# One-core, two-block transformer kernel: inputs laid out on the host, first transfers reordered, idle matmuls at the start

## The chip, the cores and the metric

The kernel runs on one core of one Trainium2 chip. The metric is device time in microseconds (us) of one execution; lower is better.

## The reference, cut to what matters

Two transformer blocks of two layers each run one after the other on one sequence of 256 tokens with 1024 features, all in float32. Layer by layer they use different mixers:

```
x = first_block(x, ...)    # layer 0: MoBA + forgetting attention; layer 1: differential + sliding-window
return second_block(x, mem_2, ...)   # layer 0: MLA, layer 1: stick-breaking; each + cross attention + MLP

h = rmsnorm(x, norm_gain[layer])
proj = h @ w_in_ab[0]                # 1024 x 4104: q,k,v,gate (4 x 512) twice, and 8 forget columns
...
h = h + mem_cross_attn(rmsnorm_2(h, norm_cross[i]), rmsnorm_2(mem, norm_mem[i]), w_q, w_kv, w_o)
h = h + sq_relu_mlp(rmsnorm_2(h, norm_mlp[i]), mlp_w_in[i], mlp_w_out[i])
```

With 256 tokens every weight is read once and used for 256 rows, so the kernel streams 155 MB of weights through the core while the matrix engine works on them.

## The kernel before, in words

The whole program is first described as a list of operations (`describe`, L1667), then `Plan.schedule` (L261) plays it through with a table of assumed costs and fixes, for each engine and for the DMA queue on SP, the order in which instructions are issued. Nothing of that model runs on the chip: there each engine works through its row and waits at semaphores for its inputs and for buffers to come free.

Activations live transposed, as eight chunks of 128 features by 256 tokens. To come near float32 with the faster `fp32r` matmul, every operand is split into a high part `hi` (a rounding copy) and a low part `lo = raw - hi`, and a product is three matmuls: hi·hi, hi·lo, lo·hi. A weight piece is 128 x 1024 float32 (512 KB). `wtiles` (L636) asks for it, `wpiece` (L619) loads it into a buffer `raw` of the pool `k4`, and `split` (L632) makes hi (mostly on ScalarE) and lo (on VectorE). `k4` has five buffers, three for `raw` and two for `fraw` (the pieces of `mem_kv`); the plan lends them to each other. A piece feeds 12 matmuls with 512 columns (token-major outputs, `proj_tok`) or 24 with 256 (feature-major, `proj_feat`). VectorE's `lo` is the last reader of `raw`, so it frees the buffer for the next load.

Source rows: a piece takes 512 columns of two 128-row chunks, so a partition receives two runs of 2 KB. The pieces of `xa_w_kv_2` (`mem_kv`, L1455) have runs of 512 B and 1 KB.

`setup` (L740) loads x token-major in four tiles `xin` and the first gain vector as eight rows, turns both around with matmuls against the identity, and takes the sum of squares with ScalarE (`squares`, L817). Sixteen transposes make x; `mem_setup` (L1430) does the same for the memory (16 more). The other gain vectors come through `rows_T` (L727): one small load per vector into rows, then one transpose. `forget` (L1118) loads the eight forget columns as 1024 runs of 32 bytes. In `describe` order: `setup`, `layer_ab`, `setup_late`, `setup_rope`, `mem_setup`, then the next layers; with loads ready from the start, the plan is free to issue those of the late setups early.

DMAs are issued from SP in one row. The program hands the completion semaphores out in turn; there are eight (DMAHW0 to DMAHW7), and from the ninth transfer on a DMA waits for the transfer that last used its semaphore.

The lines in which the buffers are set:

```python
POOLS = {"k4": (1024, 5), "k2": (512, 33), "r2": (512, 46), ...
TAGS = {"raw": ("k4", 3), "fraw": ("k4", 2), "hi": ("r2", 12), "lo": ("r2", 16), ...
```

Of the kernel before, what the change touches and what calls it, by code (L numbers as in the profile page):

```python
# [165 lines left out]
class Plan:  # L166
    def __init__(self, nc):
        self.nc = nc
        self.ops, self.tags, self.pools = [], {}, {}
# [91 lines left out]
    def schedule(self):  # L261
# [19 lines left out]
        for b in {b for o in ops for b in o.news}:  # L281
            self.tags[b.tag]["pool"].use[b.first:b.last + 1] += 1
# [36 lines left out]
        while n < len(ops):  # L319
# [69 lines left out]
            if o.kind == "dma_start":  # L389
# [4 lines left out]
                o.start, o.end = t, st + d + 1500  # L394
# [71 lines left out]
class _Eng:  # L466
# [5 lines left out]
    def __getattr__(self, method):  # L472
        plan, e = self.plan, self.e

        def call(*args, deps=(), **kw):
# [3 lines left out]
            for p in deps:  # L479
# [86 lines left out]
WEL = 1024  # L566
SUB = 512
# [13 lines left out]
PREFER = {"A": 0.0, "V": 800, "G": 1000000.0}  # L581


class Net:
# [34 lines left out]
    def wpiece(self, src, f, pat, fill="", parts=1, **kw):  # L619
# [3 lines left out]
        self.nc.sync.dma_start(raw.rearrange(pat, **kw), src)  # L623
# [12 lines left out]
    def wtiles(self, w, k0, nk, c0, nc_, fill=""):  # L636
# [3 lines left out]
        while k < k0 + nk:  # L640
# [5 lines left out]
            for hi, lo in self.wpiece(w[k * 128:(k + n) * 128, c0:c0 + nc_].rearrange("(c p) n -> p c n", p=128),  # L646
                                      n * nc_, "p (c n) -> p c n", fill, n // m, c=n):
# [91 lines left out]

    def setup(self):  # L740
        nc, a = self.nc, self.a
        rows = self.t2([8, 128], "rows")
        xin = [[self.t2([128, 512], "xin") for _ in range(2)] for _ in range(NT)]
        nc.boost = 4e4
        nc.sync.dma_start(rows, a["norm_gain"].rearrange("l (c p) -> (l c) p", p=128)[0:8])
        for hf in range(2):
            nc.boost = 1e4 if hf else 3e4
            for t in range(NT):
                nc.sync.dma_start(xin[t][hf], a["x"][0, t * 128:(t + 1) * 128, hf * 512:(hf + 1) * 512])
# [13 lines left out]
        p = self.ps("T")  # L763
        nc.tensor.transpose(p[:, :8], rows, self.ident[:8, :8])
        g0 = self.sm([128, 8], "g0")
        nc.vector.tensor_copy(g0, p[:, :8])

        self.x = self.new_x()
        self.xt = self.new_T()
        for c0 in range(0, NC8, 2):  # L770
            p = self.ps("T").rearrange("p (c n) -> p c n", c=2)
            for t in range(NT):
                for c in range(2):
                    self.tr(p[:, c, t * 128:(t + 1) * 128],
                                xin[t][c0 // 4][:, (c0 % 4 + c) * 128:(c0 % 4 + c + 1) * 128])
            for c in range(2):
                self.evac_split(self.xt[0][c0 + c], self.xt[1][c0 + c], p[:, c], g0[:, c0 + c:c0 + c + 1])
            self.copy(self.x[c0 // 2], p)
        self.stats_x(self.squares(xin))
# [25 lines left out]

        parts = []
        for i, n in enumerate("qk"):
            for j, m in enumerate(("moba", "fox", "diff", "swa")):
                gg = a[f"{m}_{n}_gain"]
                parts.append((4 * i + j, bass.AP(tensor=gg.tensor, offset=gg.offset,  # L810
                                                 ap=[[64, 1], [0, 2], [1, 64]]), 1, "p (r d) -> p r d"))
        g64 = self.rows_T("sm", 8, parts)
        self.gqk = self.sm([128, 4], "gqk")
        nc.vector.scalar_tensor_tensor(self.gqk, g64[:, 0:4], 0.125, g64[:, 4:8], op0=OP.mult, op1=OP.mult)
        self.bfor = self.bc("bfor", "sm", a["b_forget"], 8)

    def squares(self, x):  # L817

        nc = self.nc
        s2 = self.sm([128, NT, 2], "ss2")  # L820
        for t in range(NT):
            for hf in range(2):
                nc.scalar.activation(self.t2([128, 512], "sq"), x[t][hf], AF.Square, accum_out=s2[:, t, hf:hf + 1])
        ss = self.sm([128, NT], "ss")
# [903 lines left out]
```

## Time and the profile before

| | |
|---|---|
| median of 3 runs | 967.68 us (966.92 to 969.37) |
| the profiled execution | 969.73 us, of which the span from first to last instruction is 968.0 us |
| TensorE busy in the span | 940.2 us (97%), 6829 matmul records |
| VectorE, ScalarE, GpSimd busy | 679.3, 573.7, 57.9 us |
| DMA | 154.89 MB read from HBM, mean 161 GB/s |

The profiled execution is 2.05 us above the median of the runs. A busy TensorE is not one at full pace: matmuls overlap, so the pace is read from how many follow each other in a stretch without idle time. A float32 (not fp32r) matmul appears as two records, a transpose as one.

### The profile page before, as it was taken

Reading aid. Unit: us, or ns where it says so; the run is one execution under the profiler, and the core shown is the slowest. Engines: PE = TensorE matmul, PEld = TensorE weight load, DVE = VectorE, ACT = ScalarE, POOL = GpSimd, SP = SyncE. Lnnn points to the kernel's source line nnn. Section 1 sums busy time; section 2 is a strip of 40 time slices with the busy share of each in tenths; the row PEclk is TensorE's granted clock in tenths of the full one; section 3 lists DMA queues with packets and bytes.
Section 4 is the critical chain, followed back from the end, with each engine's and each line's share of the span. In section 5 each row is a group of like instructions: output and inputs, shape, how many; then the busy total and the mean of one; then the engine's idle time right before and its main releaser. Section 6 shows DMA issues by size and latency. Waiting matters only on the chain.

```text
span 968.0 us, 18191 instructions
## 1 busy us (share of the span) xinstructions
PE 940.2 (97%) x6829; PEld 869.6 (90%) x6829; DVE 679.3 (70%) x1565; ACT 573.7 (59%) x1311; POOL 57.9 (6%) x96
## 2 busy tenths in 40 slices
PE   7899999999999999999999999999999999999997
PEld 5577889889989999999999999999899999999985
DVE  7689797797988857885555556846758776666654
ACT  5667784566777765874544546535756754444453
POOL 2214000041301100000000000000000000000000
PEclk9999999999999999999999999999999999999999
DMA  7987535644514534645455566446526355555641
GB/s 189 284 213 196 129 110 174 197 131 133 160 40 117 162 111 152 211 161 171 160 172 174 178 199 222 127 155 211 168 73 197 132 175 172 176 179 193 194 154 44
DMA packets 96677, 157.13 MB, mean 162 GB/s; under 512 B 9830, under 2 KB 28492, under 8 KB 96588
## 3 DMA queue, kind: packets, MB, share of 16 engines
q1 hardware_dynamic: 96236, 154.91, 51.7%
q0 software_dynamic: 352, 1.06, 0.4%
q8 instruction: 53, 0.87, 0.4%
q14 instruction: 36, 0.29, 0.1%
HBM read 154.89 MB, written 1.06 MB: 161 GB/s over the span
## 4 chain that ended last, share of the span: by engine, by line
PE 76%; DMA 12%; DVE 6%; ACT 3%; issue 1%; SPq 1%; POOL 1%; POOLq 0%; DVEq 0%; ACTq 0%
PE psum L552 76%; DMA k<-in_w_in_ab_dram 7%; DVE r L552 3%; DMA k<-in_mlp_w_out_dram 2%; DVE k L552 2%; ACT r L552 2%; ACT k L552 1%; DMA k<-in_sb_w_qkv_dram 1%; SPq L552 1%; POOL k L552 1%; DMA k<-in_xa_w_kv_dram 1%; DMA k<-in_mlp_w_in_dram 1%; DMA k<-in_xa_w_o_dram 0%; DMA k<-in_xa_w_q_dram 0%; DMA k<-in_mla_w_uq_dram 0%
## 5 line engine op out<-in xcount | busy, mean ns | idle before, releaser
L552 PE MATMUL psum<-r,r 128*128 128x256 f32 (+1 forms) x6018 | 882.8, 304 | 9.6 <-ACT r L552 7.9
L552 PEld LDWEIGHTS psum<-r,r 128*128 128x128 f32 x6018 | 794.2, 189 | 62.3 <-ACT r L552 12.0
L552 DVE TENSOR_TENSOR r<-k,r 128x512 fp32r<-128x512 f32 (+2 forms) x669 | 409.4, 649 | 147.9 <-ACT r L552 72.1
L552 ACT ACTIVATE r<-k 128x512 fp32r<-128x512 f32 (+3 forms) x567 | 311.2, 592 | 206.2 <-PE psum L552 100.4
L552 PE MATMUL psum<-k,k 128*128 128x128 f32 (+8 forms) x771 | 132.9, 307 | 11.2 <-DVE k L552 5.4
L552 ACT ACTIVATE k<-psum 128x256 f32<-128x256 f32 (+5 forms) x171 | 71.5, 453 | 111.2 <-PE psum L552 109.1
L552 PEld LDWEIGHTS psum<-k,k 128*128 128x128 f32 (+3 forms) x771 | 92.0, 166 | 27.3 <-DVE k L552 7.4
L552 POOL TENSOR_TENSOR k<-k,k 128x2 f32<-128x2 f32 (+3 forms) x42 | 48.7, 1173 | 861.6 <-DVE k L552 860.4
L552 ACT ACTIVATE k<-k 128x256 f32<-128x256 f32 (+4 forms) x149 | 72.1, 506 | 17.9 <-DVE k L552 13.9
L552 ACT ACTIVATE k<-k,k 128x128 f32<-128x128 f32 (+3 forms) x143 | 60.7, 448 | 11.0 <-DVE k L552 7.1
L552 DVE CAST r<-k 128x512 fp32r<-128x512 f32 (+2 forms) x102 | 40.7, 403 | 28.7 <-PE psum L552 10.3
L552 DVE TENSOR_TENSOR k<-psum,k 128x512 f32<-128x512 f32 (+2 forms) x53 | 33.4, 636 | 14.9 <-PE psum L552 14.8
L552 DVE TENSOR_TENSOR k<-k,k 128x512 f32<-128x512 f32 (+4 forms) x86 | 40.2, 480 | 1.6 <-ACT k L552 0.8
L552 ACT ACTIVATE r<-k,k 128x256 fp32r<-128x256 f32 x64 | 29.7, 500 | 18.4 <-DVE k L552 16.8
L552 DVE TENSOR_TENSOR k<-k 128x256 f32<-128x256 f32 (+3 forms) x38 | 12.9, 341 | 38.4 <-ACT k L552 38.2
L552 DVE SCALAR_TENSOR_TENSOR r<-k,k,r 128x256 fp32r<-128x256 f32 x72 | 34.4, 495 | 3.0 <-ACT r L552 2.1
L552 DVE TENSOR_TENSOR r<-psum,r 128x256 fp32r<-128x256 f32 (+1 forms) x52 | 24.0, 481 | 15.1 <-ACT r L552 14.7
L552 ACT ACTIVATE r<-psum 128x256 fp32r<-128x256 f32 (+1 forms) x49 | 20.9, 435 | 16.3 <-PE psum L552 15.7
L552 DVE TENSOR_SCALAR k<-k,k 128x8 f32<-128x8 f32 (+7 forms) x97 | 24.5, 281 | 5.0 <-POOL k L552 4.5
L552 ACT ACTIVATE k<-psum,k 128x512 f32<-128x512 f32 (+1 forms) x19 | 12.1, 650 | 6.7 <-PE psum L552 6.7
L552 DVE CUSTOM_DVE_ANT_0 k<-psum,k 128x256 f32<-128x256 f32 (+1 forms) x48 | 14.7, 352 | 1.0 <-PE psum L552 1.0
L552 ACT ACTIVATION_READ_ACCUMULATOR k<-k,k 128x1 f32 x80 | 15.2, 190 | 0.0
(40 smaller groups left out, 160.3 us busy)
## 6 DMA issues: line engine op xcount, KB each, us to landing
k<-in_mlp_w_in_dram SPq DMA_DIRECT2D x64, 512.0 KB, 4.4
k<-in_mlp_w_out_dram SPq DMA_DIRECT2D x64, 512.0 KB, 5.2
k<-in_w_in_ab_dram SPq DMA_DIRECT2D x32, 512.0 KB, 6.2
k<-in_w_in_cd_dram SPq DMA_DIRECT2D x26, 512.0 KB, 4.1
k<-in_sb_w_qkv_dram SPq DMA_DIRECT2D x24, 512.0 KB, 4.5
k<-in_xa_w_kv_dram SPq DMA_DIRECT2D x16, 512.0 KB, 5.6
k<-in_w_out_ab_dram SPq DMA_DIRECT2D x8, 512.0 KB, 3.7
k<-in_w_out_cd_dram SPq DMA_DIRECT2D x8, 512.0 KB, 4.5
```

What stands on the lines that cost most here:

```text
L552: return getattr(eng, method)(*[real(a) for a in args], **{k: real(v) for k, v in kw.items()})
```

## The change

- The host lays out x and the memory transposed in chunks of 128 features, so that both are loaded straight into their tiles; the 32 transposes, their copies and `squares` go. Sums of squares are now taken by `stats_sum`, as for every other norm; for the memory the factor 1/rms is applied to keys and values after their matmuls (`rmem_bc`, `rmem`).
- All gain vectors, the forget bias and the sinks come in one 128 x 110 array `consts`, by one DMA. `rows_T` goes, and 19 small loads with it.
- `Packed` records the weight pieces in the order in which the program asks for them, and the host writes each as one contiguous block: a partition receives one run of 4 KB (the forget columns one of 256 B).
- The plan's model: a DMA may be issued only up to 4 us (`AHEAD`) ahead of its modelled data, and lands 3.0 instead of 1.5 us after them. `gate` lets the loads of the memory, of `xa_w_kv_2`, of the forget columns and of a few constants be placed only behind the copies of the first key projection, and those of the final gain behind the copies in `x_tok`. These rules act on the order of issue alone.
- Six float32 matmuls on the iota tile `dj` stand first on TensorE; nothing reads their result.

```diff
@@ class Plan
+            if o.kind == "dma_start" and dma_free > t + AHEAD:
+                heapq.heappush(fut[e], (dma_free - AHEAD, c, i))
+                continue
...
-                o.start, o.end = t, st + d + 1500
+                o.start, o.end = t, st + d + 3000
...
-            for p in deps:
+            for p in deps if plan.gate is None or method != "dma_start" else (*deps, plan.gate):
...
+    def take(self, f, cut):
+        off = sum(128 * p[0] for p in self.pieces)
+        at = self.at
+        self.pieces.append((f, lambda w: cut(w[at])))
+        return bass.AP(tensor=self.ap.tensor, offset=self.ap.offset + off, ap=[[f, 128], [1, f]])
...
-        self.nc.sync.dma_start(raw.rearrange(pat, **kw), src)
+        self.nc.sync.dma_start(raw, w.take(f, cut))
...
@@ setup
-        rows = self.t2([8, 128], "rows")
-        xin = [[self.t2([128, 512], "xin") for _ in range(2)] for _ in range(NT)]
-        nc.boost = 4e4
-        nc.sync.dma_start(rows, a["norm_gain"].rearrange("l (c p) -> (l c) p", p=128)[0:8])
-        for hf in range(2):
-            nc.boost = 1e4 if hf else 3e4
-            for t in range(NT):
-                nc.sync.dma_start(xin[t][hf], a["x"][0, t * 128:(t + 1) * 128, hf * 512:(hf + 1) * 512])
+        cst = nc.tile([128, 110], "c128", "cst")
+        self.x = self.new_x()
+        nc.boost = 5e4
+        nc.sync.dma_start(cst, a["consts"])
+        for b in range(4):
+            nc.boost = (4e4, 1e4, 3e3, 3e3)[b]
+            nc.sync.dma_start(self.x[b], a["x"][:, 2 * b:2 * b + 2])
...
+        p = self.ps("T")
+        for i in range(WARM):
+            nc.tensor.matmul(p[:, 0:256], dj[:, 0:128], dj, start=True, stop=True)
...
-            self.copy(self.x[c0 // 2], p)
-        self.stats_x(self.squares(xin))
+        self.xt = self.gained(self.x, 0)
+        nc.boost = -2e4
+        self.stats_x()
...
@@ layer_ab
+                nc.gate = self.late = nc.seen
                 c, ncb = self.forget(w, xt)
+                nc.gate = None
...
@@ mem_setup
+        self.memT = [self.t2([128, 2, 256], "memT") for _ in range(4)]
+        for b in range(4):
+            nc.sync.dma_start(self.memT[b], self.a["mem_2"][:, 2 * b:2 * b + 2])
+        self.rmem = self.rms(self.memT)
+        self.rmem_bc = self.rstd_bc(self.rmem)
...
@@ mem_kv
-            self.evac_split(kT[0][b], kT[1][b], ps)
+            y = self.t2([128, 256], "xy")
+            self.nc.vector.tensor_tensor(y, ps, self.rmem_bc, op=OP.mult)
+            self.split(y, kT[0][b], kT[1][b])
```

SP's row at the start of the program, before: behind the loads of x and the first three weight pieces (128x2x512) stand the forget columns (128x8x8), the forget bias and seven gain vectors, with one weight piece among them. The names after "waits" are the semaphores that an entry waits for.

```order
L552 DMA k_90<-in_w_in_ab_dram 128x2x512
L552 DMA k_96<-in_w_in_ab_dram 128x2x512
L552 DMA k_100<-in_w_in_ab_dram 128x8x8 [waits DMAHW0_49]
L552 DMA k_104<-in_b_forget_dram 128x8 [waits DMAHW1_49]
L552 DMA k_106<-in_moba_q_gain_dram 1x2x64 [waits DMAHW2_49]
L552 DMA k_106<-in_fox_q_gain_dram 1x2x64 [waits DMAHW3_49]
L552 DMA k_106<-in_diff_q_gain_dram 1x2x64 [waits DMAHW4_49]
L552 DMA k_106<-in_swa_q_gain_dram 1x2x64 [waits DMAHW5_49]
L552 DMA k_106<-in_moba_k_gain_dram 1x2x64 [waits DMAHW6_49]
L552 DMA k_120<-in_w_in_ab_dram 128x2x512 [waits DMAHW7_49]
L552 DMA k_106<-in_fox_k_gain_dram 1x2x64 [waits DMAHW0_49]
L552 DMA k_106<-in_diff_k_gain_dram 1x2x64 [waits DMAHW1_49]
```

SP's row at the start of the program, of the change:

```order
L558 DMA k_64<-in_consts_dram 128x110
L558 DMA k_70<-in_x_dram 128x512
L558 DMA k_77<-in_w_in_ab_dram 128x1024
L558 DMA k_80<-in_x_dram 128x512
L558 DMA k_83<-in_w_in_ab_dram 128x1024
L558 DMA k_87<-in_x_dram 128x512
L558 DMA k_89<-in_w_in_ab_dram 128x1024
L558 DMA k_94<-in_x_dram 128x512
L558 DMA k_110<-in_w_in_ab_dram 128x1024 [waits DMAHW0_49]
L558 DMA k_120<-in_w_in_ab_dram 128x1024 [waits DMAHW1_49]
L558 DMA k_77<-in_w_in_ab_dram 128x1024 [waits DMAHW2_49,DVE_49]
L558 DMA k_83<-in_w_in_ab_dram 128x1024 [waits DMAHW4_49,DMAHW3_49,DVE_49]
```

The first twelve entries now hold seven weight pieces instead of three, in all five buffers, and from the eleventh entry on the wait for VectorE (a buffer that `lo` has to free) is among them. The first weight piece is the third transfer instead of the fourth.

SP's row some entries further on, of the change, where the loads behind `gate` come:

```order
L558 DMA k_142<-in_w_in_ab_dram 128x64 [waits DMAHW5_49]
L558 DMA k_144<-in_diff_lambda_dram 128x256
L558 DMA k_110<-in_w_in_ab_dram 128x1024 [waits DMAHW7_49,DMAHW0_49,DVE_49]
L558 DMA k_149<-in_positions_dram 128x2
L558 DMA k_151<-in_mem_dram 128x512 [waits DMAHW1_49]
L558 DMA k_120<-in_w_in_ab_dram 128x1024 [waits DMAHW2_49,DVE_49]
L558 DMA k_154<-in_mem_dram 128x512 [waits DMAHW3_49]
L558 DMA k_157<-in_mem_dram 128x512 [waits DMAHW4_49]
L558 DMA k_160<-in_mem_dram 128x512 [waits DMAHW5_49]
L558 DMA k_77<-in_w_in_ab_dram 128x1024 [waits DMAHW6_49,DVE_49]
L558 DMA k_83<-in_xa_w_kv_dram 128x1024 [waits DMAHW7_49,DVE_49]
L558 DMA k_89<-in_xa_w_kv_dram 128x1024 [waits DMAHW0_49,DVE_49]
```

The memory now comes behind nine weight pieces of `w_in_ab` and before the eleventh; before the change it came behind eight of them and 22 small transfers.

TensorE's first rows, before (128x128 are the transposes of x, k_68 is the identity, 128x512 the first projection):

```order
L552 MATMUL psum_84<-k_68,k_64 128x8
L552 MATMUL psum_93<-k_68,k_69 128x128 x2
L552 MATMUL psum_98<-k_68,k_69 128x128 x2
L552 MATMUL psum_93<-k_68,k_76 128x128 x2
L552 MATMUL psum_98<-k_68,k_76 128x128 x2
L552 MATMUL psum_114<-k_68,k_82 128x128 x2
L552 MATMUL psum_115<-r_111,r_105 128x512
L552 MATMUL psum_117<-r_111,r_105 128x512
L552 MATMUL psum_119<-k_68,k_82 128x128 x2
L552 MATMUL psum_114<-k_68,k_87 128x128 x2
```

TensorE's first rows, of the change:

```order
L558 MATMUL psum_71<-k_65 128x256 x6
L558 MATMUL psum_106<-r_103,r_100 128x512
L558 MATMUL psum_108<-r_103,r_100 128x512
L558 MATMUL psum_106<-r_105,r_100 128x512
L558 MATMUL psum_108<-r_105,r_100 128x512
L558 MATMUL psum_106<-r_103,r_101 128x512
L558 MATMUL psum_108<-r_103,r_101 128x512
```

The six idle matmuls (on k_65, the iota) stand first, the transposes are gone, and the first projection matmul needs only the high parts of the first weight piece (r_103) and of the first x tile (r_100).

## Rows read from the trace of the kernel before

**Rows 1.** The page: engines' busy time; VectorE's costliest group (lo parts).

```profile
PE 940.2 (97%) x6829; PEld 869.6 (90%) x6829; DVE 679.3 (70%) x1565; ACT 573.7 (59%) x1311; POOL 57.9 (6%) x96
...
L552 DVE TENSOR_TENSOR r<-k,r 128x512 fp32r<-128x512 f32 (+2 forms) x669 | 409.4, 649 | 147.9 <-ACT r L552 72.1
```

**Rows 2.** Windows: stretch, its length, busy us of each engine, PEclk, DMA share, GB/s.

```profile
0.00:10.00 10.00, 3.18 (x12) 2.31 (x13) 8.00 (x22) 5.19 (x11) 5.09 (x46) 1.00 0.75 233
50.00:75.00 25.00, 24.07 (x117) 18.94 (x116) 21.26 (x56) 17.09 (x33) 4.32 (x3) 1.00 0.81 210
75.00:100.00 25.00, 23.52 (x160) 19.67 (x159) 22.62 (x75) 18.51 (x42) 10.41 (x8) 1.00 0.77 190
100.00:940.00 840.00, 832.75 (x6298) 784.32 (x6295) 590.82 (x1337) 498.21 (x1150) 31.41 (x33) 1.00 0.50 160
940.00:968.00 28.00, 21.01 (x99) 17.05 (x98) 10.79 (x21) 9.66 (x25) 1.10 (x2) 0.92 0.10 38
```

**Rows 3.** Timeline of TensorE, 9 to 60 us: start, length, count, idle before.

```profile
9.63 1.20 PE L552 MATMUL psum<-r,r 128*128 128x512 f32 x2
...
11.76 12.97 PE L552 MATMUL psum<-r,r 128*128 128x512 f32 x50
27.65 4.83 PE L552 MATMUL psum<-r,r 128*128 128x512 f32 x13 [2.91 <-ACT r L552]
...
47.34 13.00 PE L552 MATMUL psum<-r,r 128*128 128x512 f32 x55 [1.43 <-ACT r L552]
```

**Rows 4.** Timeline of SP's queue, 0 to 110 us: start, length of issue.

```profile
6.04 3.46 SPq L552 DMA_DIRECT2D k<-in_b_forget_dram  x1
...
12.73 0.40 SPq L552 DMA_DIRECT2D k<-in_w_in_ab_dram  x1
...
23.48 3.09 SPq L552 DMA_DIRECT2D k<-in_mem_dram  x3
```

**Rows 5.** The chain that ended last, its first long piece.

```profile
4.93 8.55 DMA k<-in_w_in_ab_dram
```

**Rows 6.** TensorE's groups by form, 8 to 14 us, then 14 to 24.7.

```profile
L552 PE MATMUL psum<-r,r 128*128 128x512 f32 x7 | 3.7, 670 | 0.0
...
L552 PE MATMUL psum<-r,r 128*128 128x512 f32 x46 | 11.1, 401 | 0.0
```

**Rows 7.** Windows of 2 us in the first 30 us, columns as in rows 2.

```profile
2.00:4.00 2.00, 0.45 (x2) 0.39 (x3) 2.00 (x5) 0.25 (x2) 1.59 (x7) 1.00 0.86 265
4.00:6.00 2.00, 1.05 (x5) 0.65 (x5) 2.00 (x5) 0.66 (x3) 2.00 (x29) 1.00 0.84 185
6.00:8.00 2.00, 0.96 (x4) 0.56 (x4) 1.83 (x7) 1.86 (x5) 0.14 (x2) 1.00 0.98 332
...
12.00:14.00 2.00, 2.00 (x6) 1.55 (x6) 1.48 (x4) 2.00 (x6) 0.00 (x0) 1.00 0.31 19
...
28.00:30.00 2.00, 2.00 (x6) 1.53 (x5) 0.92 (x2) 0.12 (x1) 0.00 (x0) 0.52 1.01 288
```

**Rows 8.** Timeline of ScalarE and VectorE, 0 to 24 us: the first weight split.

```profile
3.77 0.63 ACT L552 ACTIVATE k<-k 128x512 f32<-128x512 f32 x1 [1.75 <-DMA k<-in_x_dram]
...
8.63 0.63 ACT L552 ACTIVATE r<-k 128x512 fp32r<-128x512 f32 x1 [0.63 <-DMA k<-in_w_in_ab_dram]
...
8.97 0.48 DVE L552 SCALAR_TENSOR_TENSOR r<-psum,k,r 128x256 fp32r<-128x256 f32 x1
```

**Rows 9.** The page's DMA issues: count, KB each, median us to landing.

```profile
k<-in_mlp_w_in_dram SPq DMA_DIRECT2D x64, 512.0 KB, 4.4
...
k<-in_xa_w_kv_dram SPq DMA_DIRECT2D x16, 512.0 KB, 5.6
```

**Rows 10.** Transposes at full pace (timeline, 706 us); 128x1 matmuls by form.

```profile
706.51 1.70 PE L552 MATMUL psum<-k,k 128*128 128x128 f32 x10
...
L552 PE MATMUL psum<-k,k 128*128 128x1 f32 x32 | 4.3, 221 | 0.0
```

**Rows 11.** Who waited for whom: total us, times, longest us.

```profile
PE psum L552 <- ACT r L552: 7.9, 8, 2.9
```

More of the change, by code (lines that the diff above doesn't have):

```diff
@@ L566 @@
 WEL = 1024
+WARM = 6
 SUB = 512
@@ L581, with __init__, __getitem__, fill @@
 PREFER = {"A": 0.0, "V": 800, "G": 1000000.0}
+class Packed:
+    def __init__(self, ap, pieces=None, at=()):
+        self.ap, self.at = ap, at
+        self.pieces = [] if pieces is None else pieces
+    def __getitem__(self, l):
+        return Packed(self.ap, self.pieces, (l,))
+    def take(self, f, cut):
[3 more added lines that the diff above has]
+        return bass.AP(tensor=self.ap.tensor, offset=self.ap.offset + off, ap=[[f, 128], [1, f]])
+    def fill(self, w):
+        flat = np.concatenate([np.ascontiguousarray(cut(w)).reshape(128 * f) for f, cut in self.pieces])
+        assert flat.size == w.size
+        return flat
+def rows(k0, n, c0, nc_):
+    return lambda w: w[k0 * 128:(k0 + n) * 128, c0:c0 + nc_].reshape(n, 128, nc_).transpose(1, 0, 2)
 class Net:
@@ L762, in setup @@
         nc.gpsimd.memset(self.onec, 1.0)
[L763 to L777, printed above, removed]
-            self.copy(self.x[c0 // 2], p)
-        self.stats_x(self.squares(xin))
+        self.gcol = cst[:, 0:86]
+        self.bfor, self.sink = cst[:, 94:102], cst[:, 102:110]
+        self.xt = self.gained(self.x, 0)
+        nc.boost = -2e4
+        self.stats_x()
+        nc.boost = 0.0
         self.mask = nc.tile([128, 256], "c256", "mask")
@@ L804, in setup @@
                                 compare_op=OP.is_gt, fill=NEG, base=0, channel_multiplier=-1)
[L806 to L812, printed above, removed]
-        self.gqk = self.sm([128, 4], "gqk")
[L814 to L824, printed above, removed]
-        nc.vector.tensor_tensor(ss, s2[:, :, 0], s2[:, :, 1], op=OP.add)
-        return ss
+        self.gqk = self.sm([128, 4], "gqk")
+        nc.vector.scalar_tensor_tensor(self.gqk, cst[:, 86:90], 0.125, cst[:, 90:94], op0=OP.mult, op1=OP.mult)
     def bc(self, name, tag, ap, n):
@@ L1358, in mla, with heads @@
             self.copy(kpT[s][64 * s:64 * s + 64], p[64 * s:64 * s + 64, :256])
[L1360 to L1362 removed]
+        wq = a["mla_w_uq_2"][0]
+        def heads(b, h0, n, d0, d1):
+            return lambda w: w[b * 128:(b + 1) * 128].reshape(128, 8, 192)[:, h0:h0 + n, d0:d1]
+        wr = [next(self.wpiece(wq, heads(b, 0, 8, 128, 192), 512)) for b in range(3)]
         qp = []
@@ L1375, in mla @@
         for g in range(2):
-            wn = [next(self.wpiece(wq[b * 128:(b + 1) * 128, 4 * g:4 * g + 4, 0:128], 512, "p (h d) -> p h d", d=128))
-                  for b in range(3)]
+            wn = [next(self.wpiece(wq, heads(b, 4 * g, 4, 0, 128), 512)) for b in range(3)]
             qn, kn, v = [], [], []
@@ L1387, in mla @@
                 self.copy(qn[b2].rearrange("p h n -> p (h n)"), ps)
-            wv = [[[u.rearrange("p (h r d) -> p h r d", r=2, d=128) for u in hl] for hl in self.wpiece(
-                wk[b * 128:(b + 1) * 128, g * 1024:(g + 1) * 1024].rearrange("p (h r d) -> p h r d", r=2, d=128), 1024,
-                "p (h r d) -> p h r d", parts=2, r=2, d=128)] for b in range(2)]
+            wv = [[[u.rearrange("p (h r d) -> p h r d", r=2, d=128) for u in hl]
+                   for hl in self.wpiece(wk, rows(b, 1, g * 1024, 1024), 1024, parts=2)] for b in range(2)]
             for b2 in range(2):
@@ L1599, in finish @@
         y = {}
+        nc.gate = None
         for hf in range(2):
@@ L1669, in describe @@
     n.layer_ab()
+    n.nc.gate = n.late
     n.setup_late()
@@ L1672, in describe @@
     n.mem_setup()
+    n.nc.gate = None
     n.next_norm(8)
     n.layer_cd()
+    n.nc.gate = n.late
     n.mem_kv(0)
+    n.nc.gate = None
     n.next_norm(16)
@@ L1681, in describe @@
     n.mlp(0)
+    n.nc.gate = n.late
     n.mem_kv(1)
+    n.nc.gate = None
     n.next_norm(24)
@@ L1722 @@
                                     kind="ExternalInput").ap()
+    for name in _WEIGHTS:
+        w = np.asarray(inputs[name])
+        args[name] = Packed(nc.dram_tensor(f"in_{name}_dram", (w.size,), mybir.dt.from_np(w.dtype),
+                                           kind="ExternalInput").ap())
     out = nc.dram_tensor("out_0_dram", _OUT_SHAPE, F32, kind="ExternalOutput").ap()
```

104 lines of the change are left out of this document (40 added, 64 removed).

## The prediction

> **What bounds the kernel now.** I read the busy times first. TensorE is busy for 940.2 of 968.0 us [rows 1], so the change can win only what TensorE loses: idle time, time at a low clock, and instructions that go away. The windows say where the idle time is [rows 2]: 6.82 us in the first ten, 0.93 and 1.48 us in the two stretches from 50 to 100 us, 7.25 us in the 840 us from 100 to 940, and 6.99 us in the tail, which the change leaves as it is. The timeline adds two gaps of 2.91 and 1.43 us that end at 27.65 and 47.34 us [rows 3]. So over half of what can be won lies in the first 50 us.
>
> The pace comes from a stretch without gaps: 55 matmuls of 512 columns in 13.00 us, 0.236 us each [rows 3]. A weight piece (12 such matmuls) therefore keeps TensorE busy for 2.83 us. The first such matmul starts at 9.63 us, and up to 24.73 us (11.76 + 12.97) there are 2 + 50 of them [rows 3], which is 12.3 us of work; 12.5 us are something else: waiting, the transposes of x, and a slow start. The first seven of them last 670 ns on the mean and the next 46 last 401 [rows 6].
>
> Why TensorE runs dry at 24.73 us is to be read in SP's queue [rows 4]. Behind the first three weight pieces the forget columns go out and take 8.55 us to land [rows 5]; the issue of the forget bias lasts 3.46 us from 6.04 us on, gain vectors follow, and the fourth piece goes out at 12.73 us [rows 4]. A transfer has to wait for the one eight places ahead of it, and most of the eight are small. From 12 to 14 us the DMA engines are 0.31 busy and move 19 GB/s [rows 7]: weights are missing later because SP stood still, not because the wires were full.
>
> **The change, part by part.** The sum is made against the profiled execution of 969.73 us.
>
> (a) The first 24.73 us. In the new order the first piece is the third transfer: 0.056 MB of constants, 0.26 MB of x and the piece itself are 0.84 MB, where before 1.05 MB had to move. In 2 us at 265 and 2 us at 185 GB/s [rows 7] 0.53 and 0.37 MB move, so 0.84 MB are through at 5.7 us and 1.05 MB at 6.45. Before, ScalarE starts on the piece at 8.63 us [rows 8], 2.2 us behind that. The same lag puts the new start at 7.9 us, and the high part (0.63 us) at 8.6. I take 8.7 us for the first matmul. The transposes of x no longer stand among the matmuls. VectorE then has 0.96 us for x (2 x 0.48 us [rows 8]), 0.65 for the sum of squares and 1.3 for two low parts [rows 1]: 2.9 us per piece while x comes in, against TensorE's 2.83. They run side by side; I allow 0.3 us.
>
> The idle matmuls cost nothing, since TensorE has nothing else before the first piece; without that cover each would cost some 0.35 us. What they may bring is the clock. The PEclk column shows 1.00 from the first row of the start to the last, up to 28 us [rows 7], by which they would bring 0. The durations say otherwise: 670 against 401 ns [rows 6], and 50 matmuls in 12.97 us instead of 11.8. The nearest row for a clock that did fall is the stretch behind the 2.91 us gap: PEclk 0.52 [rows 7], 13 matmuls in 4.83 us instead of 3.07, a loss of 1.76. I take the durations, and a loss of 0.4 us that is left, between 0 (clock up from the first piece) and 1.76 (it falls again between the idle matmuls and the first piece). The Trainium skill ("TensorE: Matmul & The Clock Gate", Part 1) has half rate as the state that a core starts from, and by it the durations are right and the column is wrong here.
>
> So 9.4 us instead of 12.5 are not work: 3.1 us won. Bounds: 0.8 (first matmul at 9.63 as now, and the whole 1.76), 6.1 (bytes at 332 GB/s from 2 us on, and the lag of the first x tile, which is used at 3.77 us [rows 8]: first matmul near 6.1). The Trainium skill ("DMA: Bandwidth & Descriptors", Anatomy of one DMA) gives a transfer 2.0 us plus its bytes at 436 GB/s, measured for GpSimd's queue. By that the piece is there at 4.7 us, the first matmul comes at 5.5, (a) would be 6.3 and the time 952; no row shows a first piece landing so soon, so I stay with the rows.
>
> (b) 24.73 to 32.48 us: the gap of 2.91 us and the 1.76 us of low clock behind it, 4.67 together. In the new order seven pieces stand in the first twelve entries and none waits for a small transfer of the 32-byte kind. I take 4.3, bounds 0 and 4.67.
>
> (c) 40 to 100 us: 1.43 + 0.93 + 1.48 = 3.84 us of idle time. The first ends on a weight split [rows 3]; of the other 2.41, which lie in the attention too, I count a third. I take 2.2, bounds 0 and 3.84.
>
> (d) Instructions on TensorE behind the start. Sixteen transposes of the memory and three small ones go; ten transposes take 1.70 us at full pace [rows 10], so 2.7 + 0.5. Added are four 128x1 matmuls (two records of 0.134 each [rows 10], 1.1 us) and two 128x128 ones for `rmem_bc` (0.7, as two records at the pace of a transpose). Net 1.4 us; bounds 0.5 and 2.7.
>
> (e) 100 to 940 us. ScalarE's splits end 7.9 us of idle time in all [rows 11]; less 2.91 and 1.43, some 3.6 lie behind 50 us. Runs of 4 KB should land sooner: the pieces of `xa_w_kv_2` with runs of 512 B and 1 KB take 5.6 us, those with 2 KB 4.4 [rows 9]. The plan now expects a later landing, so a split stands less often ahead of its data. I take 1.2, bounds 0 and 3.6.
>
> What costs nothing: eight multiplications by `rmem_bc` on VectorE (under 0.65 us each, 5 us at most, and it is busy 590.82 of 840 us [rows 2]); if VectorE were the limit there, those 5 us would be paid. The gate and `AHEAD` put no wait on the chip, they only move entries. SP's row is what they move: the memory's four transfers stand between weight pieces, with ScalarE's and VectorE's splits waiting behind them.
>
> Sum: 3.1 + 4.3 + 2.2 + 1.4 + 1.2 = 12.2 us; 969.73 - 12.2 = 957.5 profiled. The profiled execution lay 2.05 us above the median, so the forecast is **955.5 us**. All bounds at once would give 946.8 and 966.4.
>
> **Rivals.**
>
> The supply fails again, later (0.14). In the new row 1.05 MB of memory and the first `xa_w_kv_2` pieces stand between the tenth and the twelfth piece of `w_in_ab`. At 332 GB/s [rows 7] the memory takes 3.2 us and two pieces another 3.2. If TensorE has no piece in hand by then, 6.4 us and once more 1.76 us of low clock come back. For it: memory tiles lie in the same queue now, where three issues last 3.09 us [rows 4]. Against it: TensorE takes 2.83 us for a piece that moves in 1.6, so the queue should be ahead of it by then. 12.2 - 8.2 = 4.0 us won, 963.7.
>
> The change doesn't do what it says (0.06). If the queue stood still for its bytes and not for small runs, (b), (c) and (e) stay, and (a) is at its lower bound: 0.8 + 1.4 = 2.2 us, 965.5, no change that can be told. Against it: the DMA engines stood at 0.31 from 12 to 14 us [rows 7], with work for them behind SP's wait.
>
> Slower (0.04): a landing in contiguous 512 KB blocks that takes longer, not shorter. A buffer is held for issue 0.4, landing, two high parts 1.2 and the last low part 0.65. With three buffers a piece comes every (landing + 2.2) / 3 us; it falls behind TensorE's 2.83 from a landing of 6.3 us on. Each us more costs 0.33 us for each of some 290 pieces, 97 us, so from 6.4 us on the gain is gone, and 6.6 us would give some 984. Against it: longer runs landed sooner [rows 9]. No row shows runs of 4 KB.
>
> **How the numbers follow.** The forecast's case has 0.76, with 949 to 960 as its own range. The range of 947.5 to 964 reaches to the first rival and leaves out the two others (0.10) and some of the ends of the first two cases. Faster by over 0.3% (2.9 us, about what this measurement can tell from no change) means below 964.8: 0.76 and most of the first rival, 0.89. Same: 0.07, slower 0.04.
>
> **What would show it.** (a): the first 512-column matmul between 8 and 9.5 us and its first seven near 400 ns. (b): no gap over 1 us between 10 and 40 us, PEclk 1.00 there, and a weight piece issued at least every 3 us. (c): under 2 us idle from 40 to 100. (d): 30 fewer 128x128 matmuls. (e): `mlp_w_in` landing below 4.4 us, and under 6.5 us idle from 100 us to the tail. The prediction is wrong if the first matmul still comes after 9.6 us, if a gap stands behind the memory's loads, or if idle time from 100 us on grows: the plan is made anew, and with it every row behind the start.

## The result and the profile after

| | before | after |
|---|---|---|
| median | 968.17 us (966.92 to 969.37, 4 runs) | 955.38 us (954.92 to 956.03, 4 runs) |
| the profiled execution | 969.73 us | 955.43 us |
| its span | 968.0 us | 953.7 us |

The ratio is 0.9868, with a 95% interval of 0.9851 to 0.9886: 1.3% faster. The forecast was 955.5 us. The two profiled executions differ by 14.30 us, where the sum of the prediction had 12.2. The profiled execution of the change lies 0.05 us above its median; that of the kernel before lay 2.05 us above its own.

The page of the changed kernel, engines' busy time, answers to [rows 1]:

```profile
PE 937.4 (98%) x6818; PEld 870.0 (91%) x6818; DVE 671.0 (70%) x1544; ACT 576.7 (60%) x1322; POOL 56.0 (6%) x96
```

Its windows, columns as in [rows 2]:

```profile
0.00:10.00 10.00, 6.07 (x15) 4.66 (x16) 7.71 (x23) 4.65 (x9) 4.21 (x45) 0.92 0.76 239
10.00:50.00 40.00, 40.00 (x189) 31.52 (x187) 34.73 (x79) 32.62 (x68) 0.00 (x0) 0.98 0.77 262
50.00:75.00 25.00, 24.00 (x142) 19.86 (x141) 23.07 (x70) 18.65 (x39) 19.61 (x14) 1.00 0.51 168
75.00:100.00 25.00, 24.48 (x155) 20.59 (x156) 22.59 (x77) 17.10 (x47) 1.05 (x2) 1.00 0.54 163
100.00:926.00 826.00, 821.73 (x6226) 776.16 (x6226) 572.07 (x1279) 494.00 (x1140) 30.00 (x34) 1.00 0.51 163
926.00:953.70 27.70, 21.07 (x101) 17.18 (x99) 10.78 (x22) 9.65 (x25) 1.10 (x2) 0.94 0.10 39
```

From 10 to 50 us TensorE is never idle; before, the two gaps of [rows 3] stood there. From 100 us to the tail it is idle for 4.27 us, where [rows 2] had 7.25. The timeline of TensorE in the first 80 us shows three idle times, of which the second, 2.70 us, is the one that matters (in brackets, idle time before and what ended it):

```profile
1.23 4.71 PE L558 MATMUL psum<-k 128*128 128x256 f32 x12 [1.23 <-POOL k L558]
8.63 19.97 PE L558 MATMUL psum<-r,r 128*128 128x512 f32 x80 [2.70 <-ACT r L558]
...
74.05 0.92 PE L558 MATMUL psum<-k,k 64*128 64x128 f32 x6 [1.00 <-DVE k L558]
```

The six idle matmuls (twelve records) end at 5.94 us, and TensorE then stands still for 2.70 us. TensorE's groups by form, first of 8 to 14 us, then of 14 to 24.7 us, answer to [rows 6]:

```profile
L558 PE MATMUL psum<-r,r 128*128 128x512 f32 x17 | 5.6, 499 | 2.7 <-ACT r L558 2.7
...
L558 PE MATMUL psum<-r,r 128*128 128x512 f32 x49 | 11.3, 389 | 0.0
```

Windows of 2 us, columns as in [rows 7], say why the first ones are slow: the granted clock (third column from the end) falls to 0.60 and 0.54 behind the 2.70 us, and is back at 1.00 from 12 us on. The trace's own clock records have it at the lower of its two levels, 1.2 of 2.4 GHz, from 8.4 to 11.8 us; TensorE had stood still from 5.94 us on.

```profile
2.00:4.00 2.00, 2.00 (x7) 1.56 (x6) 2.00 (x6) 0.00 (x0) 1.44 (x7) 1.00 0.74 160
...
8.00:10.00 2.00, 1.36 (x3) 1.12 (x4) 1.45 (x4) 2.00 (x6) 0.00 (x0) 0.60 1.05 420
10.00:12.00 2.00, 2.00 (x6) 1.53 (x5) 2.00 (x5) 2.00 (x5) 0.00 (x0) 0.54 1.03 414
12.00:14.00 2.00, 2.00 (x10) 1.64 (x10) 2.00 (x5) 2.00 (x5) 0.00 (x0) 1.00 1.02 416
```

ScalarE's timeline, which answers to [rows 8], has something that the prediction did not see:

```profile
5.34 1.28 ACT L558 ACT_TABLE_LOAD   x1 [5.34 <-DMA k<-in_x_dram]
6.64 0.91 ACT L558 ACTIVATE r<-k,k 128x256 fp32r<-128x256 f32 x2
7.45 0.61 ACT L558 ACTIVATE k<-k 128x512 f32<-128x512 f32 x1
7.97 1.13 ACT L558 ACTIVATE r<-k 128x512 fp32r<-128x512 f32 x2
```

The load of ScalarE's function table now stands behind the wait for the first x tile, and the split of x, its square and the first weight split (7.97 us) follow it in a row. SP's queue, as in [rows 4], issues nothing but weights from 5.37 to 15.93 us:

```profile
5.37 10.56 SPq L558 DMA_DIRECT2D k<-in_w_in_ab_dram  x6
15.98 0.42 SPq L558 DMA_DIRECT2D k<-in_diff_lambda_dram  x1
17.12 0.33 SPq L558 DMA_DIRECT2D k<-in_w_in_ab_dram  x1
```

Landings, and then the waits, answer to [rows 9] and [rows 11]. The page's DMA issues:

```profile
k<-in_mlp_w_in_dram SPq DMA_DIRECT2D x64, 512.0 KB, 4.2
...
k<-in_w_in_ab_dram SPq DMA_DIRECT2D x32, 512.0 KB, 4.7
...
k<-in_xa_w_kv_dram SPq DMA_DIRECT2D x16, 512.0 KB, 4.6
```

Of the waits for ScalarE's splits one is left, the one at the start:

```profile
PE psum L558 <- ACT r L558: 2.7, 1, 2.7
```

### The profile page after: what moved, and what is told of

Same layout as the page of the kernel before. It is cut to its first block, busy times and chain, and to the rows that moved or that the text cites. A ratio compares the mean times of both kernels' runs of the same rounds, so it can differ in the third digit from the quotient of the medians.

```text
span 953.7 us, 18145 instructions
## 1 busy us (share of the span) xinstructions
PE 937.4 (98%) x6818; PEld 870.0 (91%) x6818; DVE 671.0 (70%) x1544; ACT 576.7 (60%) x1322; POOL 56.0 (6%) x96
## 4 chain that ended last, share of the span: by engine, by line
PE 91%; DVE 4%; ACT 1%; DMA 1%; issue 1%; POOL 1%; POOLq 0%; SPq 0%; DVEq 0%; ACTq 0%
PE psum L558 91%; DVE r L558 2%; DVE k L558 2%; DMA k<-in_w_in_ab_dram 1%; ACT r L558 1%; ACT k L558 1%; POOL k L558 0%; DMA k<-in_x_dram 0%; ACT L558 0%; POOL cd L558 0%; POOLq L1733 0%; SPq L558 0%; DVEq L558 0%; POOLq L558 0%; ACTq L558 0%
## 5 line engine op out<-in xcount | busy, mean ns | idle before, releaser
L558 ACT ACTIVATE r<-k 128x512 fp32r<-128x512 f32 (+2 forms) x606 | 327.3, 591 | 149.1 <-PE psum L558 104.8
L558 ACT ACTIVATE k<-psum 128x256 f32<-128x256 f32 (+4 forms) x166 | 69.1, 449 | 144.5 <-PE psum L558 143.0
L558 PE MATMUL psum<-k,k 128*128 128x128 f32 (+8 forms) x748 | 126.1, 304 | 3.5 <-DVE k L558 2.4
L558 ACT ACTIVATE k<-k 128x256 f32<-128x256 f32 (+5 forms) x151 | 72.6, 505 | 16.5 <-DVE k L558 14.3
L558 ACT ACTIVATE k<-k,k 128x256 f32<-128x256 f32 (+2 forms) x144 | 60.7, 446 | 15.4 <-DVE k L558 13.5
L558 DVE TENSOR_TENSOR k<-k 128x256 f32<-128x256 f32 (+3 forms) x36 | 12.5, 352 | 54.3 <-ACT k L558 54.3
L558 DVE TENSOR_TENSOR k<-psum,k 128x512 f32<-128x512 f32 (+2 forms) x61 | 36.8, 608 | 14.4 <-PE psum L558 13.9
L558 DVE TENSOR_TENSOR k<-k,k 128x512 f32<-128x512 f32 (+5 forms) x92 | 44.2, 492 | 1.2 <-POOL k L558 0.9
L558 DVE CAST r<-k 128x512 fp32r<-128x512 f32 (+2 forms) x71 | 27.8, 395 | 14.2 <-ACT k L558 9.5
L558 DVE TENSOR_TENSOR r<-psum,r 128x256 fp32r<-128x256 f32 (+1 forms) x36 | 17.8, 508 | 13.8 <-ACT r L558 12.7
L558 DVE TENSOR_SCALAR k<-k,k 128x128 f32<-128x128 f32 (+6 forms) x94 | 22.9, 272 | 6.1 <-POOL k L558 5.5
L558 DVE TENSOR_REDUCE k<-k 128x8 f32<-128x512 f32 (+2 forms) x21 | 11.4, 571 | 5.3 <-ACT k L558 5.2
```

Of the source, the lines that this page charges most:

```text
L558: return getattr(eng, method)(*[real(a) for a in args], **{k: real(v) for k, v in kw.items()})
```

## The experiments

The theory: the gain comes from the order of the first transfers (no small loads between the weight pieces), and the contiguous blocks and the idle matmuls add little. The first rival: the blocks make it, by landing sooner. The second: the planner's new assumptions make it. Each experiment is the changed kernel with one edit, unless it says otherwise. All were compared with the kernel before on the same chip; its medians there were 968.4 to 969.2 us, against 968.17 beside the change itself. So between kernels that were timed on different chips a difference under 1 us says nothing.

**No idle matmuls, and twelve.** (`e1_no_idle`, `e2_idle12`)

```diff
-WARM = 6
+WARM = 0
```

The other kernel has 12.

> The changed kernel without the six idle matmuls. First theory: in the changed kernel TensorE idles 2.70 us between them and the first piece and the clock column shows 0.60 and 0.54 from 8 to 12 us, so they bring nothing: 955.4 us, within 0.7, first seventeen 512-column matmuls again near 500 ns. Rival: they shorten the slow stretch; then 956.5 to 958.

> The changed kernel with twelve idle matmuls. First theory: the second six run at full pace (about 0.36 us each) and end near 8.1 us, the gap before the first piece is under 1 us, the clock stays up, and the 1.6 us of slow matmuls go: 953.8 us, the first matmuls near 390 ns. Rival: the clock falls anyway or never rose: 955.4. A third way: they run past the first piece: 956 or more.

Without them: 955.77 us (955.39 to 956.14), ratio 0.9862 (0.9849 to 0.9876). With twelve: 954.13 us (953.67 to 954.80), 0.9846 (0.9832 to 0.9860). TensorE's timeline and two 2 us windows with twelve:

```profile
1.23 7.15 PE L558 MATMUL psum<-k 128*128 128x256 f32 x24 [1.23 <-POOL k L558]
8.63 11.68 PE L558 MATMUL psum<-r,r 128*128 128x512 f32 x49 [0.25 <-ACT r L558]
```

```profile
8.00:10.00 2.00, 1.75 (x7) 0.86 (x6) 1.45 (x4) 2.00 (x6) 0.00 (x0) 1.00 1.04 417
10.00:12.00 2.00, 2.00 (x11) 1.63 (x10) 2.00 (x5) 2.00 (x5) 0.00 (x0) 1.00 1.04 419
```

The first weights come at the same 8.63 us, but only 0.25 us of idle time stand ahead of them, and the clock stays at 1.00. The six idle matmuls of the change bring nothing that can be told (955.77 against 955.38 us): they end too early. By the clock records they bring the full clock at 5.0 us, lose it at 8.4 and have it again at 11.8; without them it comes at 12.3 us, and with twelve at 4.7 us to stay. Twelve bring 1.2 us over six by the medians, and 1.6 us over none on the same chip.

**Weights in their old layout.** (`e3_old_layout`) Runs of 2 KB, 1 KB, 512 B and, for the forget columns, 32 B, all else as in the change.

```diff
-        off = sum(128 * p[0] for p in self.pieces)
...
-        return bass.AP(tensor=self.ap.tensor, offset=self.ap.offset + off, ap=[[f, 128], [1, f]])
+        return cut(self.ap[self.at[0]])
```

> The changed kernel with the weights in their old layout (runs of 2 KB, 1 KB and 512 B, forget columns in 32-byte runs but behind the gate). Order theory: SP's order and the few small loads made the gain, so little is lost: 956 to 958 us, weight pieces landing 0.3 to 1 us later. Block theory: contiguous blocks made it: 961 us or more, with gaps on TensorE back in the first 60 us.

956.23 us (955.49 to 956.52), ratio 0.9866 (0.9852 to 0.9880). Its first 80 matmuls:

```profile
8.63 21.23 PE L558 MATMUL psum<-r,r 128*128 128x512 f32 x80 [3.06 <-ACT r L558]
```

No gap behind the first weights, and 0.9 us lost over the whole kernel by the medians, although the pieces of `w_in_ab` land in 6.0 us on the median instead of 4.7, and those of `xa_w_kv` in 5.7 instead of 4.6. What is lost stands in the line above: the 80 matmuls take 21.23 instead of 19.97 us, because the low clock lasts from 7.7 to 14.5 us in this execution. The first rival falls: the shorter landing is real, but pieces are asked for early enough to hide it.

**The small loads put back.** (`e5_forget32`, `e9_small_loads`) The forget columns again in 1024 runs of 32 bytes, ninth in SP's row; in the second kernel eight one-row loads behind them as well (nothing reads their data), so that the fourth weight piece is sixteenth in the row, as before the change (the last three lines of the diff).

```diff
-        nc.sync.dma_start(raw.rearrange("p c n -> p (c n)"), w.take(64, rows(0, NC8, 4096, 8)))
+        src = w.take(64, lambda m: m[:, 4096:4104])
+        nc.sync.dma_start(raw, bass.AP(tensor=src.tensor, offset=src.offset, ap=[[8, 128], [1024, NC8], [1, 8]]))
...
-                nc.gate = self.late = nc.seen
+                self.late = nc.seen
...
+        small = self.t2([8, 110], "small")
+        for i in range(8):
+            nc.sync.dma_start(small[i:i + 1], a["consts"][i:i + 1])
```

> The change, but the eight forget columns are loaded as before (1024 runs of 32 bytes) and not gated: they stand ninth in SP's row, right behind x and the first three weight pieces, and no small load follows them. If the gap of 2.91 us before came from the whole bunch of small loads among the first twenty entries, this single one delays at most the entry eight places behind it, which has its data time anyway: 0 to +1 us, about 956, no gap over 1 us between 10 and 40 us. If the 32-byte runs themselves hold up the DMA engines (8.55 us for one transfer before), the fourth and fifth piece come late: a gap of 2 to 3 us near 16 to 25 us, with a low clock behind it, and 958 to 960.

> The change with the small loads put back where they stood before: the forget columns as 1024 runs of 32 bytes ninth in SP's row, and behind them eight loads of one row of the constants (their data is not read), six of them ahead of the fourth weight piece, which is sixteenth again. All else is the change's. If the gap before came from SP standing still behind these loads, it comes back: the fourth piece goes out near 11 to 13 us, TensorE runs dry near 20 to 25 us for 2 to 4 us with a low clock behind it, and 959 to 962. If it came from the bytes that x and its transposes wanted, no gap over 1 us, and 956 to 957.

With the forget columns: 956.93 us (955.40 to 957.26), ratio 0.9880 (0.9865 to 0.9896), no gap from the first weights to 100 us. With the eight loads: 962.19 us (961.69 to 963.98), 0.9942 (0.9928 to 0.9956), which is the time that the order theory asked for, but not its mechanism. (Its profiled execution took 963.98 us, the longest of six.) SP does stand still as expected, for 5.97 us:

```profile
5.36 5.97 SPq L558 DMA_DIRECT2D k<-in_consts_dram  x6
11.77 0.36 SPq L558 DMA_DIRECT2D k<-in_w_in_ab_dram  x1
12.17 0.57 SPq L558 DMA_DIRECT2D k<-in_consts_dram  x2
12.79 26.41 SPq L558 DMA_DIRECT2D k<-in_w_in_ab_dram  x14
```

Yet TensorE does not run dry; its first weights, with a window behind them, its window from 20 to 30 us, and the place where the time went:

```profile
8.70 10.81 PE L558 MATMUL psum<-r,r 128*128 128x512 f32 x38 [1.99 <-ACT r L558]
...
10.00:12.00 2.00, 2.00 (x6) 1.60 (x5) 2.00 (x5) 2.00 (x5) 0.00 (x0) 0.51 0.66 158
...
20.00:30.00 10.00, 10.00 (x54) 7.62 (x54) 6.85 (x12) 5.52 (x10) 0.00 (x0) 1.00 0.92 334
...
260.00:280.00 20.00, 17.21 (x104) 13.29 (x102) 14.94 (x60) 11.94 (x47) 0.68 (x3) 0.74 0.23 72
```

The loss is a wait of 2.58 us for ScalarE that ends at 263.26 us, in the middle of the kernel, and the low clock behind it (0.26 of 20 us, 5.2 us at most). That is far from the loads: the plan was made anew, and this plan happens to have that wait. The same six matmuls stand behind the largest wait of `e4_old_model` below. So one small load costs some 1.5 us by the medians, which the intervals do not tell from nothing, and a stall of 6 us ahead of the fourth piece is not enough for a gap, when the pieces behind it follow in a row. That there is no gap is what the expectation gave for its other branch, the bytes of x and its transposes. This does not show that branch either, since no run puts them back.

**The planner's assumptions.** (`e4_old_model`, `e4a_land1500`, `e4b_no_ahead`, `e10_land4500`; and the kernel before with the new assumptions, `b4_model`) The diff is that of `e4_old_model`; the others have one of its two edits, or 4500 in the place of 1500.

```diff
-AHEAD = 4000.0
+AHEAD = 1e12
...
-                o.start, o.end = t, st + d + 3000
+                o.start, o.end = t, st + d + 1500
```

> The changed kernel planned with the old assumptions (no limit ahead, landing 1.5 us behind the data). Order theory: the start keeps its gain, the idle time behind 100 us grows by 0 to 2 us: 955.4 to 957.5. Rival: the new assumptions made the gain: 960 or more.

> The change, with the planner's landing time back at 1.5 us and the 4 us limit kept. If it is the assumed landing that keeps weight splits from standing ahead of their data, this brings back most of the 8 us: 960 to 964, with the waits for ScalarE's splits back above 5 us. If it is the limit on early issue, the time stays near 955 to 957.

> The change, with landing at 3.0 us and no limit on early issue. If it is the limit that brings the 8 us (an early issue takes a buffer and a place in SP's row), 960 to 964. If it is the assumed landing, 955 to 957.

> The change with the planner's landing time at 4.5 us instead of 3.0 (1.5 gave 959.3). If a later assumed landing is what keeps weight splits from standing ahead of their data, this is as good or better: 953 to 955.5. If each plan made anew just has its own few gaps, it can lie anywhere between 953 and 961, with waits that are not those for weight splits.

> The kernel before with the planner's new model alone (4 us ahead at most, landing 3.0 us behind the data). In the changed kernel, going back to the old model cost 8 us. If the model's worth lies in the model itself, this kernel gains in the stretch behind 40 us what the prediction's (c) and (e) got, 4 to 8 us: 960 to 964, with the start's 2.91 us gap still there. If the 8 us were an accident of one plan (one gap of 4 us and its low clock), this kernel stays within 2 us of the one before: 966 to 970.

| kernel | limit, landing | median (range) | ratio (95%) |
|---|---|---|---|
| the change | 4 us, 3.0 us | 955.38 (954.92 to 956.03) | 0.9868 (0.9851 to 0.9886) |
| e4b_no_ahead | none, 3.0 us | 955.27 (953.37 to 956.68) | 0.9862 (0.9843 to 0.9881) |
| e4a_land1500 | 4 us, 1.5 us | 959.26 (958.08 to 963.05) | 0.9913 (0.9894 to 0.9933) |
| e4_old_model | none, 1.5 us | 963.35 (959.91 to 964.84) | 0.9931 (0.9912 to 0.9950) |
| e10_land4500 | 4 us, 4.5 us | 968.03 (966.38 to 969.25) | 0.9997 (0.9988 to 1.0006) |
| b4_model (old kernel) | 4 us, 3.0 us | 971.50 (970.30 to 973.47) | 1.0033 (1.0020 to 1.0046) |

In the old model's timeline the start is as in the change (first matmul at 8.49 us, no gap behind it up to 100 us), and the largest wait of the plan is this one:

```profile
262.39 1.81 PE L558 MATMUL psum<-k,k 128*128 128x128 f32 x6 [4.02 <-ACT k L558]
```

With 4.5 us it is another, with a low clock behind it, between 755 and 765 us; timeline and windows of that kernel:

```profile
755.53 2.05 PE L558 MATMUL psum<-k,k 128*128 128x128 f32 x8 [3.19 <-ACT k L558]
```

```profile
755.00:760.00 5.00, 3.94 (x16) 2.82 (x17) 4.96 (x15) 4.39 (x14) 0.00 (x0) 0.65 0.90 232
760.00:765.00 5.00, 5.00 (x31) 5.00 (x31) 2.77 (x6) 2.64 (x6) 0.00 (x0) 0.67 0.20 83
...
100.00:926.00 826.00, 816.45 (x6158) 770.27 (x6157) 559.66 (x1260) 485.92 (x1138) 34.01 (x34) 1.00 0.51 160
```

With the landing at 3.0 us the limit changes nothing. The landing has no direction: 1.5 us is worse, 4.5 us is worse still, and in the old kernel the new model costs 3 us. What differs between the plans is how much idle time each holds. In `e4_old_model` and with 4.5 us one wait of 3 to 4 us stands out. With 1.5 us and the limit (`e4a_land1500`) none behind the start is over 1.42 us, and the idle time from 100 to 926 us is 8.2 us instead of 4.27. The second rival holds only in this form: without the new numbers this kernel would have met a worse plan. Of the 11.5 us between the profiled executions with 4.5 us and with 3.0 us, 5.3 are more idle time from 100 to 926 us and 3.4 the low clock of the two windows; 2.8 stay unassigned.

In the old kernel with the new model the start still runs dry, a little later, but the clock stays at 1.00 behind it:

```profile
29.35 0.73 PE L557 MATMUL psum<-r,r 128*128 128x512 f32 x2 [1.97 <-ACT r L557]
```

**The table load early; and all improvements together.** (`e6_early_table`, `e8_all_three`)

```diff
+        nc.boost = 1e5
+        nc.scalar.activation(self.sm([128, 1], "early"), self.onec, AF.Copy)
+        nc.boost = 0.0
```

The second kernel also has `WARM = 10` and constants of 128 columns.

> The change, plus one 128x1 activation on a constant at the head of ScalarE's row (its result is not read), so that ScalarE's table load (1.28 us) no longer stands behind the wait for the first x tile. If that load is on the path to the first projection matmul, ScalarE splits x from 5.4 instead of 6.6 us on, the weight split moves from 8.0 to about 7, limited by the landing of the piece, and the first matmul comes near 7.5 instead of 8.63: 954 to 955. If the piece lands only at 8 us, nothing moves: 955.4.

> Early table load, constants with 128 columns (512 bytes a partition instead of 440) and 10 idle matmuls instead of 6. Twelve idle matmuls alone kept the clock and gave 954.1. If the table load is on the path as well, the first matmul comes near 7.5 us at full clock: 952.5 to 953.5. If the piece's landing is the limit, 954 to 954.5.

With the table load early: 952.46 us (952.36 to 953.12), ratio 0.9839 (0.9824 to 0.9853). Its ScalarE timeline, its TensorE timeline and a window:

```profile
0.73 1.28 ACT L558 ACT_TABLE_LOAD   x1 [0.73 <-PEq L1724]
...
5.36 0.91 ACT L558 ACTIVATE r<-k,k 128x256 fp32r<-128x256 f32 x2 [3.13 <-DMA k<-in_x_dram]
...
6.69 1.14 ACT L558 ACTIVATE r<-k 128x512 fp32r<-128x512 f32 x2
```

```profile
1.23 4.91 PE L558 MATMUL psum<-k 128*128 128x256 f32 x12 [1.23 <-POOL k L558]
7.36 18.82 PE L558 MATMUL psum<-r,r 128*128 128x512 f32 x80 [1.22 <-ACT r L558]
```

```profile
8.00:10.00 2.00, 1.99 (x9) 1.58 (x9) 2.00 (x6) 2.00 (x5) 0.00 (x0) 1.00 1.04 418
```

One 128x1 activation moves the weight split from 7.97 to 6.69 us and the first matmul from 8.63 to 7.36. The six idle matmuls now end only 1.22 us ahead of it, and the clock stays at 1.00: 1.3 us of earlier start and 1.1 of clock, 2.4 of the 2.9 us that it gains over the change. This is the fastest kernel of the study.

All together: 952.87 us (952.26 to 954.56), 0.9844 (0.9828 to 0.9860), no better. Ten idle matmuls took from 1.23 to 8.87 us, the first real one starts at 8.52 instead of 7.36, and the expected 7.5 was missed because the filling was too long. Its profiled execution is the longest of its four (954.56 us).

## Why the prediction was right

The forecast of the time held to 0.1 us, and that closeness is luck. The sum is 2.1 us short of the 14.30 us between the profiled executions. It was then lowered by 2.05 us, the distance of the profiled execution from the median before, which the change does not have (0.05 us). The two errors cancel. What was right is where the time would be won and, but for (e) and the unmeasured (d), about how much.

- **(a) The first 24.73 us.** The first matmul was put at 8.7 us and came at 8.63. The first seven should have lasted near 400 ns; the first 17 last 499, and the eight up to 12 us 622, hardly less than the 670 before. The step that failed is the loss of 0.4 us for the clock. The prediction named a fall between the idle matmuls and the first piece as its upper bound and did not count on it; it came, because they end at 5.94 us with 2.70 us of nothing behind them. Eighty matmuls take 19.97 us, at full pace 18.88 (80 x 0.236): 1.1 us lost, where the clock and VectorE together were given 0.7. With twelve idle matmuls the same eighty take 18.77 us, so all of it is the clock, and the 0.3 us allowed for VectorE are not there. By the same pace, 9.7 us up to 28.60 us are not work (12.5 before): 2.8 won, predicted 3.1. The reasoning on what sets 8.7 us was not right either. Bytes and a lag were taken from the old kernel, but the table load (1.28 us) was on the path; without it the first matmul comes at 7.36.
- **(b) The gap.** All of it is gone: 4.67 us won, predicted 4.3. There is no gap from 10 to 40 us and the clock is at 1.00 from 12 us on; of the signs asked for, only "a weight piece at least every 3 us" fails, twice (18.93, then 23.41 us, with three loads of the memory between; 31.75, then 37.38 us), and TensorE had pieces in hand. For the order of the transfers speaks that neither the old layout of the weights, nor the old model, nor the lack of idle matmuls brings the gap back, and that the old order keeps one under the new model. It is argued by elimination and not shown: the old loading of x with its transposes was not put back, nor were all the small loads. The step "the fourth piece goes out at 12.73 us" as the cause is not borne out: with the fourth piece at 11.77 us there is no gap. ScalarE's timeline of the kernel before, from the fourth weight split on, shows how it came about:

```profile
17.80 1.15 ACT L552 ACTIVATE r<-k 128x512 fp32r<-128x512 f32 x2 [1.81 <-DMA k<-in_w_in_ab_dram]
...
20.62 1.16 ACT L552 ACTIVATE r<-k 128x512 fp32r<-128x512 f32 x2 [1.18 <-DMA k<-in_w_in_ab_dram]
23.31 1.16 ACT L552 ACTIVATE r<-k 128x512 fp32r<-128x512 f32 x2 [1.53 <-DMA k<-in_w_in_ab_dram]
26.97 1.16 ACT L552 ACTIVATE r<-k 128x512 fp32r<-128x512 f32 x2 [2.50 <-DMA k<-in_w_in_ab_dram]
```

  From the fourth piece on every split waits for its data, so the lead is used up at 17.80 us, but TensorE runs dry only at the seventh, which SP issued at 20.66 us, behind eleven more small loads, and which ScalarE had 6.3 us later. In that stretch the DMA engines were full and slow (the window from 20 to 30 us had a share of 0.99 at 233 GB/s; after the change 344 GB/s at 0.95). Whether the lateness of its issue or the slow landing weighs more was not tried apart.

  A third thing is in the counts. Up to 24.73 us TensorE took 52 matmuls of 512 columns [rows 3]. That is four pieces of twelve and four matmuls of a fifth, while ScalarE had begun six. The plan fixes TensorE's row, and in the row that it gives the kernel before, the 53rd of these matmuls is the first on the seventh piece; eight on the fifth and all twelve on the sixth stand behind it. So TensorE waited with 20 matmuls, 4.7 us at 0.236, of pieces that were split by 25.3 us and that its row did not let it take. In the row of the change the seventh piece is first used by the 67th matmul, and in the kernel with eight small loads by the 61st. By these counts the gap took both, a late seventh piece and a row that asks for it early. That is worked out and not tried: no run changed the row alone.
- **(c) 40 to 100 us.** 1.52 us idle instead of 3.84: 2.3 won, predicted 2.2, and under the 2 us that was asked for. The plan here is a new one too, so the closeness is in part luck.
- **(d) Transposes.** TensorE has 28 records of 128x128 fewer (422 to 394, the lines below), which is the 32 transposes of x and the memory less two float32 matmuls of two records each, and eight 128x1 records more: the counts that the 1.4 us were worked out from. The time itself was not measured apart.

```profile
L552 PE MATMUL psum<-k,k 128*128 128x128 f32 x422 | 83.1, 280 | 6.9 <-DMA k<-in_x_dram 4.3 <-DVE k L552 1.4 <-POOL k L552 0.7
...
L558 PE MATMUL psum<-k,k 128*128 128x128 f32 x394 | 74.5, 274 | 1.2 <-DVE k L558 0.6 <-ACT k L558 0.5
```

- **(e) 100 us on.** 3.0 us won, predicted 1.2: the term was too small, and its reasons do not hold. Sooner landings are there, and worth under 1 us; the assumed landing matters, but in no direction that could be foretold. The measured 3.0 us lie within the bounds of 0 to 3.6, but these were too narrow for a plan that is made anew: from the table of the models, up to 12.7 us lie between plans that differ in one number. The term held its bounds because this plan is a good one.

The sum is 2.8 + 4.7 + 2.3 + 1.4 + 3.0 = 14.2 of the 14.30 us between the profiled executions. Of it 12.8 us were measured; the 1.4 of (d) are the forecast, and 1.5 us are left over for it, 0.3 of them in the tail (28.0 to 27.70 us). Of the rivals, the supply did not fail later; "it doesn't do what it says" falls with (b); slower landings fall with 4.2 and 4.7 us.

## What to carry to other kernels

Where one engine is busy 97% of the time, look for idle stretches with a clock drop behind them: three waits of 2.6 to 3.2 us cost 4.7, 6.6 and at most 7.8 us here with the clock behind them, at the start and in the middle alike. Fillers that keep the clock have to end close ahead of the first real instruction (1.22 us ahead was close enough here, 1.99 was not) and must not run past it, so shorten the wait first (a table load moved ahead of a data wait gave 2.9 us, doubling the fillers gave 1.2). Before blaming the loads for an idle engine, count what it has in hand: an engine that works through its row in order can wait for one piece while others lie ready. Where a planner orders the program, a change of a number in it is a new draw: time several such plans before crediting the number, and give the term for "everything behind" both signs.

## What the runs showed of the hardware that was not expected

- After idle matmuls, 2.70 us of idle time (the change) and 1.99 us (the kernel with eight small loads: granted clock 0.51 from 10 to 12 us) were followed by a low clock, 1.22 us and 0.25 us were not. Behind a long busy stretch 1.97 us were not either (the kernel before with the new model, granted clock 1.00 from 28 to 32 us), so the length of the idle time does not settle it alone.
- TensorE starts slowly while the PEclk column has 1.00: without idle matmuls the window from 10 to 12 us (below) has 6 records of matmuls at 1.00, with twelve idle ones 11 records at 1.00. The column cannot show the slow start: the first clock record of the trace is the rise to the full clock, at 12.3 us without idle matmuls and at 14.4 us before the change, and where no record stands the column has 1.00. The Trainium skill ("TensorE: Matmul & The Clock Gate", Part 1) has half rate as the state from which TensorE starts; the durations agree with it.

```profile
10.00:12.00 2.00, 2.00 (x6) 1.59 (x5) 2.00 (x5) 2.00 (x5) 0.00 (x0) 1.00 1.05 425
```

- The first table load takes 1.28 us, and the next activation starts right behind it (5.34 and 6.64 us). The Trainium skill ("ScalarE: Activation LUTs", What ACT_TABLE_LOAD costs) has about 1283 ns for it, which the trace confirms, and 1380 ns of drain for a switch, which this first load does not show, nor does a later one (load at 35.80 us, straight behind an activation, and the next activation at 37.09).
- Runs of 4 KB instead of 2 KB moved the median landing of one tensor (`w_in_ab`) from 6.0 to 4.7 us, and the time by less than 1 us.
